# First layer's gate: the last 22 blocks' products made in row tiles of 64 and of 32 rows

## The chip, the cores and the metric

The kernel runs on one core of a Trainium2 chip. A core has TensorE (matrix products, PE in the profile; its weight loads are listed apart as PEld), VectorE (DVE), ScalarE (ACT), GpSimd (POOL) and SyncE (SP), which work through queues of their own, and 16 DMA engines that move data between the memory of the chip and the on-chip buffer. TensorE writes its results to PSUM, which this kernel uses as eight banks of 128 partitions by 512 float32 numbers. The metric is the time of one execution in microseconds (us).

## The reference, cut to what matters

The program is a two-layer transformer-like model on 256 tokens and 256 context tokens of width 2048. The first layer is a Fourier mixer with a gate:

```
def _fourier_branch(h, w_in, w_mix):
    u, z = jnp.split(h @ w_in, 2, axis=-1)          # each [512 tokens, 4096] with the context
    ...                                             # f: FFT over tokens and groups of u, then a mix
    return f * jax.nn.silu(z)

h = _rmsnorm(x, norm_g[i]) * (1 + scale) + shift
y = _fourier_branch(h, fnet_w_in[j], fnet_w_mix[j])
x = x + gate * (y @ w_out[i])
```

The change touches how `z = h @ w_in[:, 4096:]` is computed for 22 of its 32 blocks of 128 columns. Each block is a product of a 2048 x 128 piece of the weight, transposed, with h transposed (2048 x 512, both token sets side by side). The sum over the 2048 rows is made as 16 steps (k) of 128 rows. Everything is float32 in the reference. The second layer is an attention with a gate, and then a last norm.

## The kernel before, in words

All products of the gate are made in TensorE's fp32r format. To keep the precision, each operand is split in a high part (the value cast to fp32r) and a low part (what the cast left), and a product is three matmuls: high by high, high by low, low by high. The helper `mm3` (lines 78 to 81) issues these three, and so nearly all of TensorE's work stands on lines 79, 80 and 81 in the profile. The helper `half_split` (from line 67) makes the split of 128x1024 weights: the cast on ScalarE (L69, tile `wh`) and the subtraction on VectorE (L70, tile `wl`). The split halves live in the pool `ws`, six buffers, so three halves (high and low each). The raw weights come through the pool `raw`, three buffers of 128x2048.

The gate has 32 blocks, numbered b. Six are made early in the kernel and stored (`zd`), four beside each other in the stage ahead of the change, and the last 22 (b = 10 to 31) in a loop of their own. That loop is what changes. Per block it

- loads one raw weight tile of 128x2048 (SP queue) and splits it in two halves (`ws_split`);
- loads the Fourier part `ys[b]` from DRAM, after the weight's DMA;
- takes one PSUM bank and runs 16 steps of `mm3` into it, 48 matmuls of 128 rows (K), 128 columns of weights and 512 moving columns. The operand h is kept as 16 pairs `hs[k]` of a high and a low 128x512 tile, some in the pool `hx`, the others in `act`, so the profile calls the tiles `hx` or `act`;
- calls `z_out(b, o)`: a Silu on ScalarE from PSUM into a tile `z` (L703), the product `y = y * z` on VectorE (L704), and one or two pieces of another job, `next(ada)`.

The job `ada` (L666) is the conditioning product for later stages. It is made on VectorE with fused multiply-and-sum instructions on 128x1024 pieces of weights, which come through the same three `raw` buffers. It fills VectorE's time beside the gate and goes on in the stage behind it, the first layer's output projection. That stage starts with eight PSUM banks.

The order of the instructions on each engine is made by a planner, which goes by the program's order and by simulated times; `tc.issue_after` ties some instructions behind others. In each engine's queue the order is then fixed.

Three other places are named in the prediction. Line 320 and line 1220 use TensorE in tiles smaller than the array. Line 1220 (`stage_o`, in the second layer) is the value product of the attention:

```
for b in range(16):
    for hh in range(2):
        for g in range(4):
            q = slice(g * 32, g * 32 + 32)
            PE.matmul(oo[g][hh * 64 : hh * 64 + 64, 0:N], vrep[0][q, b, :], pall[q, hh, b].rearrange(...), start=b == 0, stop=b == 15)
```

There each matmul has 32 rows (partitions q) and 64 columns of weights, with four positions of rows (g) and two of columns (hh), in plain float32, for which the trace has two records a matmul (128 matmuls a stage, eight stages, 2048 records). Line 1015 is a 128x128 transpose in float32, also with two records each.

Of the kernel before, what the change touches and what calls it, by code (L numbers as in the profile page):

```python
# [10 lines left out]
F32 = mybir.dt.float32  # L11
F32R = mybir.dt.float32r
AF = mybir.ActivationFunctionType
ALU = mybir.AluOpType
AX = mybir.AxisListType

P = 128
D = 2048
KT = D // P
# [10 lines left out]
def tile_dit(ctx: ExitStack, tc: tile.TileContext, a: dict, out: bass.AP):  # L30
    nc = tc.nc
    V, S, PE, GP = nc.vector, nc.scalar, nc.tensor, nc.gpsimd
# [8 lines left out]
    def psum():  # L41
        return pp.tile([P, 512], F32, tag="ps", name="ps")
# [35 lines left out]
    def mm3(o, wh, wl, xh, xl, start, stop):  # L78
        PE.matmul(o, wh, xh, start=start, stop=False)  # L79
        PE.matmul(o, wh, xl, start=False, stop=False)  # L80
        return PE.matmul(o, wl, xh, start=False, stop=stop).ins  # L81
# [98 lines left out]
    with tc.tile_pool(name="st", reuse_waits="tile", bufs=1, side="right") as st, ExitStack() as sts:  # L180
# [306 lines left out]
        for i in range(4):  # L487
            for j in range(4):
                k = 4 * i + j
# [38 lines left out]
    for i in range(2):  # L528
        t = act(F32R).rearrange("p (k c) -> p k c", c=64)
# [149 lines left out]
    with tc.tile_pool(name="yp", reuse_waits="tile", bufs=32) as ypool:  # L679
        ys = []  # L680
        for b in range(NB):
            y = ypool.tile([P, 512], F32, tag="y", name="y")
            ys.append(y)
        hs = []
        hs_end = [None] * 3

        def make_hs(k):
            xt = act()
            hs_end[2] = nc.gpsimd.dma_start(xt, a["xT"][:, k, :]).ins
            h, l = h_tile(k), h_tile(k)  # L690
            for s in range(2):
                q = slice(s * N, (s + 1) * N)
                t = xt[:, q]
                V.scalar_tensor_tensor(t, t, gs0[:, k, s : s + 1], r_bc[:, q], op0=ALU.mult, op1=ALU.mult)
                hs_end[1] = S.activation(h[:, q], t, AF.Identity, bias=sh0[:, k, s : s + 1]).ins
                hs_end[0] = V.scalar_tensor_tensor(l[:, q], t, sh0[:, k, s : s + 1], h[:, q].bitcast(F32), op0=ALU.add, op1=ALU.subtract).ins
            hs.append((h, l))

        with tc.tile_pool(name="zp", reuse_waits="tile", bufs=2) as zp:
            def z_out(b, o):  # L700
                y = ys[b]
                z = zp.tile([P, 512], F32, tag="z", name="z")
                S.activation(z, o, AF.Silu)  # L703
                V.tensor_tensor(y, y, z, op=ALU.mult)  # L704
                if b >= NE + 4:
                    with tc.issue_after(hs_end[0]) if b < NE + 8 else nullcontext():
                        for _ in range(2 if b % 4 == 2 else 1):
                            next(ada)

            o4 = [psum() for _ in range(4)]  # L710
            for kg in range(4):
                wr = rawp.tile([P, D], F32, tag="raw", name="raw")
                last_dma[0] = nc.sync.dma_start(wr.rearrange("p (b c) -> p b c", b=4), a["wz"][NE - 4 : NE, :, kg * 512 : (kg + 1) * 512].rearrange("b p c -> p b c")).ins
                w = []
                for i in range(2):
                    make_hs(kg * 4 + i * 2)
                    with tc.issue_after(hs_end[0]) if kg else nullcontext(), tc.issue_after(hs_end[1]) if kg else nullcontext():
                        w.append(half_split(wr, i))
                    make_hs(kg * 4 + i * 2 + 1)
                for j in range(4):  # L720
                    k = kg * 4 + j
                    for b in range(4):
                        wh, wl = w[b // 2]
                        q = slice((b % 2) * 512 + j * P, (b % 2) * 512 + (j + 1) * P)
                        mm3(o4[b], wh[:, q], wl[:, q], hs[k][0], hs[k][1], k == 0, k == KT - 1)
            for b in range(NE + 4):
                with tc.issue_after(last_dma[0]):
                    nc.sync.dma_start(ys[b], fd[b])
            for b in range(4):
                z_out(NE + b, o4[b])  # L730
            for b in range(NE):
                z = zp.tile([P, 512], F32, tag="z", name="z")
                with tc.issue_after(last_dma[0]):
                    nc.sync.dma_start(z, zd[b])
                V.tensor_tensor(ys[b], ys[b], z, op=ALU.mult)
            for b in range(NE + 4, NB):
                w = ws_split(raw(a["wz"][b - 4]))
                with tc.issue_after(last_dma[0]):
                    nc.sync.dma_start(ys[b], fd[b])
                o = psum()  # L740
                for k in range(KT):
                    wh, wl = w[k // 8]
                    q = slice((k % 8) * P, (k % 8 + 1) * P)
                    mm3(o, wh[:, q], wl[:, q], hs[k][0], hs[k][1], k == 0, k == KT - 1)
                z_out(b, o)


        x1, sqs = [], []
        yy = {}

        def y_split0(i):
            for j in range(2):
                h, l = hxt(F32R), hxt(F32R)
                split(h, l, ys[i % 16 * 2 + j])
                yy[i, j] = (h, l)

        def evac0(k, o):
            t = xin.pop(0)
            for s in range(2):
                q = slice(s * N, (s + 1) * N)  # L760
                e = V.scalar_tensor_tensor(t[:, q], o[:, q], gt0[:, k, s : s + 1], t[:, q], op0=ALU.mult, op1=ALU.add).ins
            x1.append(t)
            t2 = hxt()
            with tc.issue_after(kv_w[0]) if k == 8 else nullcontext():
                sq_end[0] = S.activation(t2, t, AF.Square).ins
            if k in (13, 14):
                late.append(t2)
            elif 0 < k < 15:
                V.tensor_tensor(sqs[0], sqs[0], t2, op=ALU.add)
            else:  # L770
                sqs.append(t2)
            if k == 15:
                with tc.issue_after(e):
                    for t2 in late:
                        add_end[0] = V.tensor_tensor(sqs[0], sqs[0], t2, op=ALU.add).ins

        late, sq_end, add_end, kv_w = [], [None], [None], []
        xin = []
        ada_rate = {2: 2, 5: 2, 8: 2, 11: 2, 15: 0, 16: 0, 19: 2, 22: 2, 25: 2, 28: 2, 30: 0, 31: 0}
        y_split0(0)  # L780
        for i in range(32):
            sw, kg = i // 16, i % 16
            if kg == 0:
                o = [psum() for _ in range(8)]
            w = ws_split(raw(a["wo0"][sw, kg]))
            if i < 31:
                y_split0(i + 1)
            if kg >= 12:
                for k in range(sw * 8 + (kg - 12) * 2, sw * 8 + (kg - 12) * 2 + 2):
                    t = act()  # L790
                    nc.gpsimd.dma_start(t, a["xT"][:, k, :])
                    xin.append(t)
            for _ in range(ada_rate.get(i, 1)):
                next(ada)
            if i == 31:
                kv_raw = raw(a["wkv"][0])
                kv_h = wsp.tile([P, 1024], F32R, tag="ws", name="wh")
                kv_l = wsp.tile([P, 1024], F32R, tag="ws", name="wl")
                kv_w.append(S.copy(kv_h, kv_raw[:, 0:1024]).ins)
            if i == 24:  # L800
                S.activation(junk[:, 0:1], epsd, AF.Sqrt)
            edge = kg in (0, 15)
            for j, b in [(j, b) for b in range(8) for j in range(2)] if edge else [(j, b) for j in range(2) for b in range(8)]:
                q = slice(b * P, (b + 1) * P)
                mm3(o[b], w[j][0][:, q], w[j][1][:, q], *yy[i, j], kg + j == 0, kg * 2 + j == NB - 1)
                if kg == 15 and j == 1:
                    evac0(sw * 8 + b, o[b])
# [18 lines left out]
    o = psum()  # L826
# [12 lines left out]
    o = psum()  # L839
# [17 lines left out]
    for s in range(2):  # L857
        o = psum()[:, 0:N]
# [28 lines left out]
    with tc.tile_pool(name="h1", reuse_waits="tile", bufs=16) as h1p:  # L887
        hx1 = []
        kT = []
        with tc.tile_pool(name="kvp", reuse_waits="tile", bufs=2) as kvp:  # L890
            hc1 = []
            for k in range(KT):
                hx = h1p.tile([P, 512], F32R, tag="h1", name="h1")
                hc = kvp.tile([P, 512], F32R, tag="h1c", name="h1c", bufs=16)
                t = kvp.tile([P, 512], F32, tag="ht", name="ht")
                for s, h in ((0, hx), (1, hc)):
                    q = slice(s * N, (s + 1) * N)
# [10 lines left out]
            o = [[psum() for _ in range(2)] for _ in range(4)]  # L908
            for kg in range(8):
                w = [(kv_h, kv_l)] if kg == 0 else ws_split(raw(a["wkv"][kg]))  # L910
                for j in range(2):
                    k = kg * 2 + j
# [3 lines left out]
                    wh, wl = w[j]  # L916
                    for tb in range(4):
                        h = (hx1, hc1)[tb // 2][k]
                        c = (tb % 2) * P
                        for kv in range(2):  # L920
                            q = slice(kv * 512, (kv + 1) * 512)
                            mm3(o[tb][kv], h[:, c : c + P], h[:, N + c : N + c + P], wh[:, q], wl[:, q], k == 0, k == KT - 1)
            kr = []
            for tb in range(4):
                t = kvp.tile([P, 512], F32, tag="v", name="v", bufs=4)
# [3 lines left out]
                t = kvp.tile([P, 512], F32, tag="kr", name="kr", bufs=4)  # L929
# [5 lines left out]
            for hp in range(4):  # L935
                o = psum()
                for tb in range(4):
                    PE.transpose(o[:, tb * P : (tb + 1) * P], kr[tb][:, hp * P : (hp + 1) * P], ident)
                t = act()
# [7 lines left out]
        with tc.tile_pool(name="ye", reuse_waits="tile", bufs=6) as yep, ExitStack() as ats:  # L947
# [344 lines left out]
            with tc.tile_pool(name="fin", reuse_waits="tile", bufs=1) as fp:  # L1292
# [41 lines left out]
                o = [[psum() for _ in range(2)] for _ in range(2)]  # L1334
# [171 lines left out]
```

## Time and profile before

| | us |
|---|---|
| median of 3 runs | 1796.85 |
| lowest, highest | 1794.87, 1797.44 |
| the profiled execution's time | 1795.95 |
| its span, first to last instruction | 1794.2 |
| stage of blocks 10 to 20, from 423.0 | 122.4 |
| stage of blocks 21 to 31, from 545.4 | 122.9 |
| PE, DVE, ACT busy, share of the span | 99%, 77%, 49% |

Times in the trace are counted from the span's start. A row of the groups reads: line, engine, operation, tile written <- tiles read, shape, count | busy us, mean ns of one | idle time of the engine just ahead of them and what ended it. A "form" row gives the shortest, the median and the longest duration in ns. Durations of matmuls and weight loads are latencies and overlap; how often one starts tells the pace. The chain of work that ended last lists what the end of the kernel hung on, in order of time.

### The profile page before, as it was taken

To read this page: it belongs to the slowest core of one execution; us is meant where nothing else is said; L and a number is where in the kernel's file an instruction comes from. 1 tells how busy PE (TensorE), PEld (TensorE's weight loads), DVE (VectorE), ACT (ScalarE), POOL (GpSimd) and SP (SyncE) were. 2 spreads that over 40 slices of the span, in tenths; PEclk is the share of its full clock that TensorE was granted. 3 is DMA by queue.
4 is the path that set the end of the run, shared out by engine and by line. 5 is a ranking of instruction groups with operands and counts; after the bars stand their busy time and mean duration, and the time that the engine had idled before them with its cause. 6 is when DMAs were issued, how large, how long until landed. Compare 5 with 4: busy or idle time off the path is not lost.

```text
span 1794.2 us, 28006 instructions
## 1 busy us (share of the span) xinstructions
PE 1769.7 (99%) x10941; PEld 1486.6 (83%) x10941; DVE 1377.9 (77%) x2314; ACT 880.4 (49%) x1530; POOL 184.2 (10%) x224
## 2 busy tenths in 40 slices
PE   8999999999999999999999999999999999999997
PEld 6669999987888888888888888888888888887886
DVE  5769999978897887696976473788888878877454
ACT  6546444543322232323332353677778767866343
POOL 0001000020000010000000001033213312301010
PEclk9999999999999999999999999999999999999999
DMA  9985555476766676654576233544344343346543
GB/s 387 420 367 176 210 200 193 165 281 233 294 254 237 252 273 254 255 211 164 190 263 224 91 141 113 187 158 151 133 153 151 144 146 138 142 165 239 195 168 137
DMA packets 69028, 370.20 MB, mean 206 GB/s; under 512 B 8736, under 2 KB 10928, under 8 KB 35360
## 3 DMA queue, kind: packets, MB, share of 16 engines
q1 hardware_dynamic: 55344, 328.51, 48.9%
q0 software_dynamic: 9520, 32.96, 5.3%
q10 hardware_dynamic: 4032, 6.95, 1.1%
q8 instruction: 86, 1.41, 0.3%
q14 instruction: 46, 0.38, 0.1%
HBM read 353.16 MB, written 15.21 MB: 205 GB/s over the span
## 4 chain that ended last, share of the span: by engine, by line
PE 97%; ACT 1%; DMA 1%; DVE 0%; issue 0%; SPq 0%; DVEq 0%; ACTq 0%
PE ps L79 26%; PE ps L81 26%; PE ps L80 25%; PE ps L1142 7%; PE ps L1220 3%; PE ps L1144 3%; PE ps L320 2%; PE ps L1173 2%; PE ps L1174 2%; PE ps L1015 0%; DMA xn<-in_x 0%; DMA x1d<-act 0%; PE ps L629 0%; PE ps L600 0%; PE ps L336 0%
## 5 line engine op out<-in xcount | busy, mean ns | idle before, releaser
L69 ACT CAST wh<-raw 128x1024 fp32r<-128x1024 f32 x178 | 186.7, 1052 | 410.3 <-PE ps L80 377.6
L70 DVE TENSOR_TENSOR wl<-raw,wh 128x1024 fp32r<-128x1024 f32 x178 | 220.1, 1238 | 146.3 <-ACT wh L69 145.8
L79 PE MATMUL ps<-hx,wh 128*128 128x512 f32 x700 | 274.5, 394 | 0.0
L81 PE MATMUL ps<-hx,wl 128*128 128x512 f32 x700 | 273.1, 393 | 0.0
L80 PE MATMUL ps<-hx,wh 128*128 128x512 f32 x700 | 273.0, 390 | 0.0
L1092 DVE TENSOR_TENSOR wl<-raw,wh 128x1024 fp32r<-128x1024 f32 x142 | 190.6, 1348 | 39.2 <-ACT wh L1086 37.6
L1142 PE MATMUL ps<-h,wh 128*128 128x512 f32 x512 | 184.0, 399 | 0.0
L666 DVE CUSTOM_DVE_ANT_0 raw<-raw,cb 128x1024 f32<-128x1024 f32 x128 | 154.8, 1219 | 30.9 <-DMA raw<-in_adw 30.2
L1086 ACT CAST wh<-raw 128x1024 fp32r<-128x1024 f32 x142 | 148.8, 1049 | 59.0 <-PE ps L80 34.2
L81 PEld LDWEIGHTS ps<-hx,wl 128*128 128x128 f32 x700 | 131.4, 188 | 31.0
L80 PEld LDWEIGHTS ps<-hx,wh 128*128 128x128 f32 x700 | 131.4, 188 | 29.6
L79 PEld LDWEIGHTS ps<-hx,wh 128*128 128x128 f32 x700 | 131.5, 188 | 27.8 <-ACT hx L405 0.8
L1144 PE MATMUL ps<-h,wl 128*128 128x256 f32 x512 | 138.6, 281 | 0.0
L666 DVE CUSTOM_DVE_ANT_0 junk<-raw,cb 128x1024 f32<-128x1024 f32 x96 | 117.1, 1220 | 22.4 <-DMA raw<-in_adw 12.5
L80 PE MATMUL ps<-wl,h 128*128 128x512 f32 x320 | 125.2, 391 | 0.0
L81 PE MATMUL ps<-wh,h 128*128 128x512 f32 x320 | 124.9, 392 | 0.0
L79 PE MATMUL ps<-wh,h 128*128 128x512 f32 x320 | 124.5, 396 | 0.2 <-ACT h L899 0.2
L1191 ACT ACTIVATE p<-ps,mx 128x512 f32<-128x512 f32 x128 | 86.8, 683 | 75.0 <-DVE mx L1182 74.4
L1142 PEld LDWEIGHTS ps<-h,wh 128*128 128x128 f32 x512 | 96.1, 188 | 21.4
L1144 PEld LDWEIGHTS ps<-h,wl 128*128 128x128 f32 x512 | 96.6, 189 | 3.0
L81 PE MATMUL ps<-act,wl 128*128 128x512 f32 x234 | 91.0, 394 | 0.7 <-DVE wl L70 0.7
L1182 DVE CUSTOM_DVE_ANT_0 ps<-ps,mask,nsink 128x512 f32<-128x512 f32 x128 | 91.1, 752 | 0.5
(366 smaller groups left out, 4014.2 us busy)
## 6 DMA issues: line engine op xcount, KB each, us to landing
raw<-in_adw SPq DMA_DIRECT2D x64, 1024.0 KB, 4.9
raw<-in_wz SPq DMA_DIRECT2D x58, 1024.0 KB, 4.8
raw<-in_awp SPq DMA_DIRECT2D x32, 1024.0 KB, 12.4
raw<-in_wo SPq DMA_DIRECT2D x32, 1024.0 KB, 4.8
raw<-in_wq SPq DMA_DIRECT2D x32, 1024.0 KB, 4.8
raw<-in_wu SPq DMA_DIRECT2D x25, 1016.0 KB, 4.9
raw<-in_wo1b SPq DMA_DIRECT2D x16, 1024.0 KB, 4.8
act<-in_xT POOLq DMA_DIRECT2D x32, 256.0 KB, 5.1
```

The costliest lines, as they stand in the source:

```text
L69: cast[0] = S.copy(h, t[:, i * 1024 : (i + 1) * 1024]).ins
L70: V.tensor_tensor(l, t[:, i * 1024 : (i + 1) * 1024], h.bitcast(F32), op=ALU.subtract)
L79: PE.matmul(o, wh, xh, start=start, stop=False)
L80: PE.matmul(o, wh, xl, start=False, stop=False)
L81: return PE.matmul(o, wl, xh, start=False, stop=stop).ins
L666: V.tensor_tensor_reduce(junk if s == 0 and i < 3 else wf, wf, cb[:, s], 1.0, 0.0, ALU.mult, ALU.add, acc[:, i, kh, fg * 2 + f, s : s + 1])
L1086: cast[0] = S.copy(h, t[:, i * 1024 : (i + 1) * 1024]).ins
L1092: V.tensor_tensor(ready[n][1], ready[n][2], ready[n][0].bitcast(F32), op=ALU.subtract)
L1142: PE.matmul(o[0], wh[:, q], hx1[k], start=k == 0, stop=k == KT - 1)
L1144: PE.matmul(o[0][:, 0:N], wl[:, q], hx1[k][:, 0:N], start=False, stop=False)
L1182: V.tensor_tensor_reduce(so[tb], so[tb], mask[:, tb, :], -0.125, nsink[:, i : i + 1], ALU.add, ALU.min, mx[:, tb : tb + 1])
L1191: S.activation(pt[:, tb, :], so[tb], AF.Exp, bias=mx[:, tb : tb + 1], scale=-1.0, accum_out=sm[:, tb : tb + 1])
```

## The change

In the loop over the last 22 blocks, the 128 rows of each step k are cut in pieces of n rows: two of 64 rows for b = 10 to 20, four of 32 rows for b = 21 to 31. Each piece has a PSUM bank of its own and sums its own rows over all 16 steps. For each of the three products of a step, the pieces follow one another, so that neighbouring matmuls use different rows of the array. The three products and their order stay the same. At the end of a block ScalarE copies the first bank to a new tile `zt` in the on-chip buffer (one buffer), VectorE adds the others to it one by one, and `z_out` works on `zt` instead of PSUM.

```diff
                 with tc.issue_after(last_dma[0]):
                     nc.sync.dma_start(ys[b], fd[b])
-                o = psum()
+                n = 64 if b < 21 else 32
+                o = [psum() for _ in range(P // n)]
                 for k in range(KT):
                     wh, wl = w[k // 8]
                     q = slice((k % 8) * P, (k % 8 + 1) * P)
-                    mm3(o, wh[:, q], wl[:, q], hs[k][0], hs[k][1], k == 0, k == KT - 1)
-                z_out(b, o)
+                    for j, (wx, hx_) in enumerate(((wh, hs[k][0]), (wh, hs[k][1]), (wl, hs[k][0]))):
+                        for i, oi in enumerate(o):
+                            rows_ = slice(i * n, (i + 1) * n)
+                            PE.matmul(oi, wx[rows_, q], hx_[rows_], start=k == 0 and j == 0, stop=k == KT - 1 and j == 2)
+                t = zp.tile([P, 512], F32, tag="zt", name="zt", bufs=1)
+                S.copy(t, o[0])
+                for oi in o[1:]:
+                    V.tensor_tensor(t, oi, t, op=ALU.add)
+                z_out(b, t)
```

Per block this is 96 matmuls of 64 rows, or 192 of 32 rows, in place of 48 of 128 rows, each with 128 columns of weights and 512 moving columns, two or four PSUM banks in place of one, one more ScalarE instruction, and one or three more on VectorE. Loads from DRAM are unchanged.

## The prediction

> **What bounds the kernel now.** I read the page first: the busy shares, the granted clock and the chain of work that ended last.
>
> ```profile
> span 1794.2 us, 28006 instructions
> PE 1769.7 (99%) x10941; PEld 1486.6 (83%) x10941; DVE 1377.9 (77%) x2314; ACT 880.4 (49%) x1530; POOL 184.2 (10%) x224
> PEclk9999999999999999999999999999999999999999
> PE 97%; ACT 1%; DMA 1%; DVE 0%; issue 0%; SPq 0%; DVEq 0%; ACTq 0%
> ```
>
> 97% of the chain is TensorE at a full clock, so a nanosecond added to each product of a stage is a nanosecond of the kernel, and the other engines matter only where they make TensorE wait. Next, the windows of the two stages that change (columns: length, busy us and instruction count of PE, weight loads, DVE, ACT, POOL; clock, DMA share, GB/s), the first the 64-row blocks, the second the 32-row blocks:
>
> ```profile
> 423.00:545.40 122.40, 121.71 (x525) 98.30 (x524) 105.22 (x157) 33.53 (x39) 0.54 (x1) 1.00 0.71 268
> 545.40:668.30 122.90, 122.90 (x531) 99.54 (x530) 101.47 (x152) 35.35 (x42) 7.17 (x14) 1.00 0.67 254
> ```
>
> Eleven blocks of 48 matmuls are 528, and 122.90/531 gives 231.5 ns from one to the next: 11.1 us a block. VectorE is busy for 101 of 123 us here, so it is the engine to watch.
>
> **Are row tiles worked on side by side?** The 22 blocks keep their 1056 products but issue each as two (528 x 2 = 1056) or four (528 x 4 = 2112) matmuls of as many columns. If the pieces ran one after the other they would cost a full pass each. The kernel already has one place with row tiles: line 1220, 32 rows by 64 columns, four row tiles times two column tiles. Its rows in the chain, and those of full-array float32 transposes (L1015) and of full-array products beside it:
>
> ```profile
> 1143.99 0.87 PE ps L1015 x8
> ...
> 1200.37 0.23 PE ps L79
> ...
> 1203.77 0.23 PE ps L1173
> ...
> 1204.68 7.72 PE ps L1220 x256
> 1212.40 0.43 PE ps L79
> ```
>
> A float32 record on the full array takes 0.87/8 = 109 ns for 128 moving columns, so 218 ns for the 256 of line 1220. 256 of them in turn would be 55.8 us; they took 7.72, 7.2 at a time. Two column tiles alone give two at a time and four row tiles alone four, so both work together here. That is the row nearest to the change, and by it I take two 64-row pieces, and four 32-row pieces, for the price of one full product.
>
> **Are their weight loads hidden too?** A load comes with every matmul, so the change doubles or quadruples the loads, each still of 128 columns. The forms (min/median/max ns):
>
> ```profile
> L1220 PEld LDWEIGHTS ps<-pall,vr x2048: 127/132/132, 1204.6 to 1642.4; 32*64 32x64 f32 x187
> L1220 PE MATMUL ps<-pall,vr x2048: 371/374/425, 1204.6 to 1642.6; 32*64 32x256 f32 x187
> L81 PEld LDWEIGHTS ps<-act,wl x234: 186/188/188, 379.9 to 667.4; 128*128 128x128 f32 x117
> L81 PE MATMUL ps<-act,wl x234: 387/393/497, 380.1 to 667.7; 128*128 128x512 f32 x117
> ```
>
> These are latencies that overlap, so only their pace says what a load occupies. Line 1220 did 256 loads of 64 columns in 7.72 us: 30.2 ns each, or 60.3 ns for 128 columns, even if one loader served all tiles. Four such loads are 241 ns against 231.5: nearly hidden if they were strictly serial, wholly if row tiles load side by side. The other end comes from the widest pace of a 128-column load for these fp32r products, beside matmuls of 256 columns:
>
> ```profile
> 142.99 0.28 PE L81 MATMUL ps<-hx,wml 128*127 128x256 f32 x1
> ...
> 143.94 0.28 PE L80 MATMUL ps<-act,wmh 128*127 128x256 f32 x1
> ```
>
> Nine starts, eight steps in 0.95 us: 119 ns, so a load occupies at most that. Two in turn are 238 ns (6 ns too many), four 475 ns (244 too many). Ends: 0 and 528 x 6 + 528 x 244 = 3 + 129 = +132 us. I take 0, because line 1220 has the same 32-row tiles and already moves 512 weight columns in 241 ns.
>
> The Trainium skill, "TensorE: Matmul & The Clock Gate", section "The mechanism" of Part 3, speaks against the change: a weight load overlaps a running matmul only when the row group differs. By that each tile would pay a load and then a stream, 60 + 231.5 ns at the least, some +64 us over 1056 products. The trace disagrees: line 1220's eight tiles each had 256/8 = 32 records in 7.72 us, 241 ns a record, where the stream alone is 218 and a serial load at the bound would bring it to 278.
>
> **Mode changes.** The first product after line 1220 stands at 0.43 us in the chain, the others at 0.23: 0.20 us for one change of tile shape. There are three (128 to 64 rows, 64 to 32, back to 128): **+0.6 us**. Ends 0 and 3 x 0.43 = 1.3.
>
> **What the sum of the pieces adds.** Each block gains one ScalarE copy of 128x512 out of PSUM and one (64-row) or three (32-row) VectorE adds from PSUM, and the Silu then reads SBUF instead of PSUM. Nearest rows, and the present work of the 32-row stage:
>
> ```profile
> L822 ACT COPY act<-ps 128x512 f32<-128x512 f32 x8 | 4.4, 583 | 2.1 <-DMA x1d<-act 2.0
> L1307 DVE TENSOR_TENSOR act<-ps,gbc 128x512 f32<-128x512 f32 x7 | 4.5, 682 | 8.0 <-PE ps L81 8.0
> L703 ACT ACTIVATE z<-ps 128x512 f32<-128x512 f32 x11 | 6.6, 596 | 30.0 <-PE ps L81 30.0
> L666 DVE CUSTOM_DVE_ANT_0 junk<-raw,cb 128x1024 f32<-128x1024 f32 x28 | 34.2, 1220 | 4.5 <-DMA raw<-in_adw 2.6 <-ACT cb L659 1.9
> L666 DVE CUSTOM_DVE_ANT_0 raw<-raw,cb 128x1024 f32<-128x1024 f32 x27 | 32.9, 1219 | 0.3
> L70 DVE TENSOR_TENSOR wl<-raw,wh 128x1024 fp32r<-128x1024 f32 x22 | 26.9, 1222 | 14.8 <-ACT wh L69 14.8
> L704 DVE TENSOR_TENSOR y<-y,z 128x512 f32<-128x512 f32 x11 | 7.6, 687 | 3.8 <-ACT z L703 3.8
> ```
>
> ScalarE: 11 x 0.58 = 6.4 us a stage on an engine busy for 35 of 123 us; nothing. VectorE, 64-row stage: 11 x 0.68 = 7.5 us into 122.4 - 105.2 = 17.2 us of free time. 32-row stage: 33 x 0.68 = 22.5 us into idle time of 4.5 + 0.3 + 14.8 + 3.8 = 23.4 us. That nearly fills VectorE. Most of that idle time is spare, for it waits on ScalarE's cast, which waits on TensorE. Behind the adds in VectorE's queue stand the low halves of the weights (L70), which TensorE needs, and behind the Silu in ScalarE's queue the next cast (L69). Their lead:
>
> ```profile
> 489.72 1.05 ACT L69 CAST wh<-raw 128x1024 fp32r<-128x1024 f32 x1 [4.51 <-PE ps L80]
> ...
> 495.30 1.05 ACT L69 CAST wh<-raw 128x1024 fp32r<-128x1024 f32 x1 [2.23 <-PE ps L80]
> ```
>
> Casts come 5.6 us apart, each released by TensorE's last read of a half. The six weight buffers hold three halves (high and low), so a half is wanted two halves later: 11.1 us, less 1.05 for the cast and 1.22 for L70, leaves 8.8 us. The new chain at a block's end (copy 0.58, three adds 2.05, Silu 0.60) delays a cast by at most 3.2 us and leaves 5.6 for VectorE to lag. I take **+2 us** of TensorE waiting; ends 0 (the lead holds) and 22.5 + 7.5 = 30 (none of the idle time usable). The first blocks have less lead. There TensorE already waited for L70 once:
>
> ```profile
> 428.90 0.50 PE L81 MATMUL ps<-act,wl 128*128 128x512 f32 x1 [0.69 <-DVE wl L70]
> ```
>
> That is in block 10, before its add, so it stays. PSUM: four banks a block in eight banks give each block 11.1 us to be copied and added (2.6 us), and the output projection behind starts on the four banks of block 30 (4 x 6 x 0.23 = 5.5 us of cover).
>
> **Sum.** The profiled execution took 1795.95 us (span 1794.2, 1.75 around it). 1795.95 + 0.6 + 2 = 1798.6; the median shown, 1796.85, is 0.9 above that execution, so 1799.4, say **1799 us**.
>
> **The rivals.**
>
> *One loader for all tiles.* The loads of row tiles take turns, at a price between the two paces, 60 and 119 ns. For: no row shows 128-column fp32r loads in row tiles. Against: line 1220's pace. It decides above 231.5/4 = 58 ns in the 32-row blocks, above 116 in the 64-row ones. Midway, at 90 ns, four are 360: 528 x 128 = 68 us, 1867 us; the end is 1799 + 132 = 1931.
>
> The Trainium skill, "TensorE: Matmul & The Clock Gate", "Measured speedup vs the span model", gives four row tiles of 32 rows and 512 columns a speedup of 3.07, not 4: an estimate of 1.30 products a set, 528 x 70 ns = +37 us, 1836. No run here shows that shape; 1.30 sets is a load of 75 ns in this rival.
>
> *The tiles take turns.* Row tiles of full 128-column width, fp32r, don't overlap: (1 + 3) x 528 x 231.5 ns = +489 us, 2288 us. For it only that line 1220 differs in type and width.
>
> *Faster: the gap between products goes.* From 256 columns in 119 ns and 512 in 226.7 (fifteen products from 1200.37 to 1203.77) a column costs 0.42 ns, so 512 stream in 215 and 16.5 of the 231.5 are gap. If tiles fill one another's gaps, 1056 x 16.5 = 17.4 us come back: 1782. For: line 1220's 7.2 at a time out of 8 includes its two ends, so it loses little in between. Against: a tile's own next product still has its own gap. From 6 ns of gap won, the kernel is faster beyond the noise.
>
> *VectorE becomes the bound.* The waits in its queue stay where they are and half of the 30 us is exposed: 1812 us. For: 22.5 into 23.4. Against: the lead of 5.6 us a half.
>
> *Instructions come late.*
>
> ```profile
> PE ps L1220 <- issue: 3.8, 3, 1.6
> q8 instruction: 86, 1.41, 0.3%
> ```
>
> The 2 x 10941 TensorE records over 86 packets are 254 each. At line 1220 a packet lasted 3.8 us and TensorE stood still three times in eight such stages, 1.6 us at the longest. The 32-row blocks issue 384 instructions in 11.1 us, a packet in 7.4: twice the time. If each of their 17 packets stalled 1.6 us: +27, 1826 us.
>
> **How the numbers follow.** Side by side, as summed: 0.50, its own range 1794 to 1806. One loader 0.20. Turns 0.12. Faster 0.10. VectorE 0.05, instructions 0.03. A measurement of this kernel tells about 0.2% (3.6 us) from no change. Faster by more: 0.09 of the gap rival, 0.02 of the forecast: 0.11. Within: 0.30 of the forecast, 0.01: 0.31. Slower: 0.18 of the forecast and all of the other four (0.40): 0.58. The range leaves out the turns (0.12) and the full gain of the gap (0.05) and goes from 1788 to 1926.
>
> **What will show it.** Both windows at 122 to 125 us with 1056 and 2112 matmuls of 64 and 32 rows: the step on tiles holds. The first unchanged and the second long, with evenly spaced matmuls: the loader. Twice and four times as long: turns. Shorter windows: the gap. TensorE waiting on L70 or on the new adds: VectorE. My weakest step is the load: fp32r loads in row tiles appear nowhere in this trace.

## The result and the profile after

The changed kernel took **1960.33 us** (median of 3 runs, 1959.86 to 1960.48) against 1796.85: 1.0912 times as long, 95% interval 1.0887 to 1.0937. That is 161 us above the forecast of 1799 and outside its range. The profile of the changed kernel, first the page's lines for the span, the busy time, the granted clock in 40 slices and the chain that ended last:

```profile
span 1958.5 us, 32285 instructions
PE 1820.0 (93%) x13053; PEld 1518.6 (78%) x13053; DVE 1410.9 (72%) x2358; ACT 887.8 (45%) x1552; POOL 184.6 (9%) x224
PEclk9999999998888878889999999999999999999999
PE 56%; issue 7%; DVE 6%; DMA 4%; ACT 1%; DVEq 0%; ACTq 0%; POOLq 0%
```

The clock is no longer full in slices 10 to 18 (441 to 881 us), which is where the change lies, and the chain that was 97% TensorE is now broken by VectorE and DMAs. The same window view as before, for the 64-row stage, the 32-row stage, and the start of the output projection behind them:

```profile
417.00:608.00 191.00, 147.46 (x1083) 114.82 (x1082) 117.21 (x176) 36.25 (x47) 0.80 (x2) 0.87 0.49 176
608.00:814.30 206.30, 150.32 (x2116) 119.57 (x2112) 120.52 (x177) 34.98 (x45) 7.48 (x14) 0.85 0.45 156
814.30:844.00 29.70, 11.31 (x33) 7.42 (x33) 20.11 (x33) 6.63 (x11) 0.54 (x1) 0.69 0.47 161
```

**Where the 164.3 us lie** (span 1794.2 to 1958.5). The two stages took 245.3 us before, from 423.0 on. They take 397.3 now, from 417.0 on, since the first products of block 10 are mixed with those of the block ahead: 152.0 - 6.0 us. The projection then stands still for 29.7 - 11.3 = 18.4 us. Together 164.4. Within the 397.3 us TensorE is idle for 43.5 + 56.0 = 99.5. At full pace the work in them is 245.3 + 6.0 = 251.3; the other 46.5 us are products at less than full pace.

**The row tiles themselves keep the pace forecast.** TensorE's timeline, one stretch in each stage (columns: start, duration, then the instruction; x4 are four neighbours drawn together):

```profile
602.60 0.63 PE L748 MATMUL ps<-act,wh 64*128 64x512 f32 x4
603.06 0.40 PE L748 MATMUL ps<-act,wl 64*128 64x512 f32 x2
603.29 0.63 PE L748 MATMUL ps<-hx,wh 64*128 64x512 f32 x4
...
612.22 0.64 PE L748 MATMUL ps<-hx,wh 32*128 32x512 f32 x8
612.69 0.40 PE L748 MATMUL ps<-hx,wl 32*128 32x512 f32 x4
612.92 0.63 PE L748 MATMUL ps<-act,wh 32*128 32x512 f32 x8
```

A step k, three products, goes from 602.60 to 603.29 and from 612.22 to 612.92: 0.69 and 0.70 us, 0.23 a product, whether it comes in two pieces or in four. Before it was 231.5 ns. From the starts of all sets in the trace, the median is 233 ns for pairs and for sets of four, those just behind a wait included; in the run with the order held (below) it is 232 for both, as in the kernel before, read in the same way.

**What TensorE waits for.** The waits between 415 and 860 us (us in all, times, longest), some rows of the list:

```profile
ACT z L703 <- DVE zt L752: 302.1, 21, 23.0
DVE junk L666 <- DMA raw<-in_adw: 128.2, 27, 7.1
PE ps L748 <- DVE wl L70: 44.9, 14, 10.6
PE ps L748 <- DVE zt L752: 43.8, 19, 11.8
PE ps L79 <- DVE zt L752: 13.6, 1, 13.6
PEld ps L748 <- issue: 1.4, 4, 0.4
```

TensorE waits for VectorE: for the low halves of weights (L70) and for the adds (L752) that free its PSUM banks. VectorE has work for only 117 and 121 us of these long stages; it waits itself, 128 us in all, at a conditioning piece (L666) for weights. (One `next(ada)` loads one tile of weights and works it off in four instructions on L666; "piece" below is one of these four.) VectorE's timeline in the middle of the two stages shows the order in which this happens:

```profile
594.54 1.22 DVE L70 TENSOR_TENSOR wl<-raw,wh 128x1024 fp32r<-128x1024 f32 x1
595.68 0.68 DVE L752 TENSOR_TENSOR zt<-ps,zt 128x512 f32<-128x512 f32 x1
597.06 0.69 DVE L704 TENSOR_TENSOR y<-y,z 128x512 f32<-128x512 f32 x1 [0.70 <-ACT z L703]
598.00 1.23 DVE L70 TENSOR_TENSOR wl<-raw,wh 128x1024 fp32r<-128x1024 f32 x1 [0.24 <-ACT wh L69]
604.16 1.23 DVE L666 CUSTOM_DVE_ANT_0 junk<-raw,cb 128x1024 f32<-128x1024 f32 x1 [4.94 <-DMA raw<-in_adw]
...
607.84 1.22 DVE L666 CUSTOM_DVE_ANT_0 raw<-raw,cb 128x1024 f32<-128x1024 f32 x1
609.22 1.22 DVE L70 TENSOR_TENSOR wl<-raw,wh 128x1024 fp32r<-128x1024 f32 x1
610.46 0.68 DVE L752 TENSOR_TENSOR zt<-ps,zt 128x512 f32<-128x512 f32 x1
```

and SyncE's queue (two issues of loads drawn as one row), the total of what its loads waited for on L70 from 415 to 860 us, and TensorE:

```profile
599.25 10.18 SPq L47 DMA_DIRECT2D raw<-in_adw  x2
```

```profile
SPq L47 <- DVE wl L70: 100.8, 24, 14.9
```

```profile
595.82 0.50 PE L748 MATMUL ps<-hx,wl 64*128 64x512 f32 x2 [3.23 <-DVE wl L70]
...
610.49 0.51 PE L748 MATMUL ps<-hx,wl 32*128 32x512 f32 x4 [1.50 <-DVE wl L70]
```

Read it as a ring. The low half at 598.00 ends at 599.23 and is the last reader of its `raw` buffer. At 599.25 SyncE issues the load of conditioning weights into a `raw` buffer. VectorE has that load's piece next in its queue and stands still until 604.16. It works off four pieces (4.9 us) and only then makes the low half at 609.22, for which TensorE has been waiting, and the add at 610.46, for which the Silu has been waiting on ScalarE and, behind the Silu, the next cast. Then the ring starts anew. A turn is 609.22 - 594.54 = 14.7 us, where a block of products is 11.1.

Not every turn is like this one. In some VectorE stands before two such loads, one behind the other:

```profile
679.07 1.23 DVE L666 CUSTOM_DVE_ANT_0 junk<-raw,cb 128x1024 f32<-128x1024 f32 x1 [5.05 <-DMA raw<-in_adw]
...
688.87 1.23 DVE L666 CUSTOM_DVE_ANT_0 junk<-raw,cb 128x1024 f32<-128x1024 f32 x1 [4.89 <-DMA raw<-in_adw]
```

Between the Silu at 452.07 and the last at 845.83 lie 21 turns. Twelve with one load take 14.4 to 16.0 us, 50 us more in all than twelve blocks at 11.1; seven with two loads take 18.1 to 28.4, 94 us more; two with a wait for `cb`, the vector that the pieces are multiplied with, 17 more. So over half of the loss is in the seven turns with two loads.

### The profile page after: what moved, and what is told of

The parts are those of the page before. It is cut to its first block, busy times and chain, and to the rows that moved or that the text cites. A ratio compares the mean times of both kernels' runs of the same rounds, so it can differ in the third digit from the quotient of the medians.

```text
span 1958.5 us, 32285 instructions
## 1 busy us (share of the span) xinstructions
PE 1820.0 (93%) x13053; PEld 1518.6 (78%) x13053; DVE 1410.9 (72%) x2358; ACT 887.8 (45%) x1552; POOL 184.6 (9%) x224
## 4 chain that ended last, share of the span: by engine, by line
PE 56%; issue 7%; DVE 6%; DMA 4%; ACT 1%; DVEq 0%; ACTq 0%; POOLq 0%
PE ps L79 13%; PE ps L81 13%; PE ps L80 13%; PE ps L1150 6%; DMA raw<-in_adw 4%; PE ps L1228 3%; PE ps L1152 3%; DVE junk L666 2%; PE ps L1181 1%; PE ps L1182 1%; DVE wl L70 1%; DVE raw L666 1%; DVE zt L752 1%; PE ps L748 1%; DMA cb<-in_crow 0%
## 5 line engine op out<-in xcount | busy, mean ns | idle before, releaser
L70 DVE TENSOR_TENSOR wl<-raw,wh 128x1024 fp32r<-128x1024 f32 x178 | 220.9, 1242 | 120.8 <-ACT wh L69 120.8
L666 DVE CUSTOM_DVE_ANT_0 junk<-raw,cb 128x1024 f32<-128x1024 f32 x96 | 117.3, 1222 | 164.6 <-DMA raw<-in_adw 138.1
L79 PE MATMUL ps<-hx,wh 128*128 128x512 f32 x546 | 216.2, 399 | 18.3 <-DVE zt L752 13.6
L81 PE MATMUL ps<-hx,wl 128*128 128x512 f32 x546 | 214.6, 395 | 0.0
L80 PE MATMUL ps<-hx,wh 128*128 128x512 f32 x546 | 214.2, 392 | 0.0
L666 DVE CUSTOM_DVE_ANT_0 raw<-raw,cb 128x1024 f32<-128x1024 f32 x128 | 155.3, 1222 | 48.0 <-DMA raw<-in_adw 46.0
L748 PE MATMUL ps<-hx,wh 32*128 32x512 f32 (+1 forms) x924 | 139.8, 443 | 48.4 <-DVE zt L752 43.8
L748 PE MATMUL ps<-act,wh 32*128 32x512 f32 (+1 forms) x1188 | 152.2, 413 | 6.2 <-ACT wh L69 6.2
L703 ACT ACTIVATE z<-zt 128x512 f32<-128x512 f32 x22 | 13.9, 631 | 312.3 <-DVE zt L752 302.1
L748 PEld LDWEIGHTS ps<-hx,wh 32*128 32x128 f32 (+1 forms) x924 | 86.7, 211 | 71.8 <-DVE zt L752 53.7
L79 PEld LDWEIGHTS ps<-hx,wh 128*128 128x128 f32 x546 | 103.9, 190 | 41.4 <-DVE zt L752 14.0
L81 PEld LDWEIGHTS ps<-hx,wl 128*128 128x128 f32 x546 | 103.7, 190 | 25.0 <-DVE wl L70 0.8
L80 PEld LDWEIGHTS ps<-hx,wh 128*128 128x128 f32 x546 | 103.7, 190 | 23.5 <-DVE hx L62 0.5
L748 PEld LDWEIGHTS ps<-act,wh 32*128 32x128 f32 (+1 forms) x1188 | 103.1, 199 | 23.8 <-ACT wh L69 7.0
```

The source lines that it names most:

```text
L70: V.tensor_tensor(l, t[:, i * 1024 : (i + 1) * 1024], h.bitcast(F32), op=ALU.subtract)
L666: V.tensor_tensor_reduce(junk if s == 0 and i < 3 else wf, wf, cb[:, s], 1.0, 0.0, ALU.mult, ALU.add, acc[:, i, kh, fg * 2 + f, s : s + 1])
L748: PE.matmul(oi, wx[rows_, q], hx_[rows_], start=k == 0 and j == 0, stop=k == KT - 1 and j == 2)
```

## The experiments

Where no interval is given, a time is that of one run; twelve runs of the kernel before lay between 1793.73 and 1797.06 us. Each row of order strings below lists one engine's queue over three or four of the 32-row blocks. VectorE: `w` a low half (L70), `a` a conditioning piece (L666), `+` an add, `y` the product behind the Silu (L704). ScalarE: `C` a cast, `K` the copy out of PSUM, `Z` the Silu.

Two theories stand at the head. A: the Silu, which used to wait for TensorE only, now waits in ScalarE's queue for VectorE's adds, and holds up the casts behind it. B: the queues are in another order than before, in which the low halves and adds stand behind conditioning pieces that wait for loads. A third, plainer one is that the sum's own work is too much for VectorE. In all experiments line numbers below the edit shift by a few.

### The sum left out

```diff
-                t = zp.tile([P, 512], F32, tag="zt", name="zt", bufs=1)
-                S.copy(t, o[0])
-                for oi in o[1:]:
-                    V.tensor_tensor(t, oi, t, op=ALU.add)
-                z_out(b, t)
+                z_out(b, o[0])
```

> The row tiles stay, two of 64 and four of 32 rows, but the copy to zt and the adds are left out: the Silu reads the first bank alone, so the gate holds only the first piece's rows (the sum over the other pieces is what this kernel leaves out). Theory A, the new wait: ScalarE's Silu now waits for VectorE's adds, and the casts that feed TensorE stand behind it in ScalarE's queue. Without the sum that wait is gone: 1796 to 1806 us. Theory B, the order: the planner, which the trace shows to have packed the conditioning job ahead of a block's second low half, made an order that fits a slower TensorE, and it is this order that starves TensorE. The order here is nearly that of the changed kernel, with the adds left out, so most of the loss stays: 1880 to 1960 us. Theory C, VectorE has too much work: 30 us of adds are gone, so near 1800.

1925.72 us, against 1794.57 for the kernel before beside it. With no copy, no add and no wait of the Silu for an add, 131 of the 165 us are still lost. Its waits from 415 to 850 us:

```profile
DVE junk L666 <- DMA raw<-in_adw: 138.0, 27, 7.2
PE ps L748 <- DVE wl L70: 79.2, 21, 11.5
```

So neither the sum nor its wait is the main cause.

### The sum made, but not read

```diff
                 for oi in o[1:]:
                     V.tensor_tensor(t, oi, t, op=ALU.add)
-                z_out(b, t)
+                z_out(b, o[0])
```

> As the changed kernel with its copy and adds, but the Silu reads the first bank in PSUM and nobody reads zt (the gate leaves the other pieces out). VectorE has all of its new work, ScalarE's Silu no longer waits for it. Theory A: the loss goes, 1797 to 1815 us. Theory B: most of it stays, 1880 to 1960. Theory C (VectorE's work): it stays as it was, 1940 to 1965.

1945.27 us. The copies and adds bring 20 us over the kernel without them, the Silu's wait for them another 15; VectorE stands still for conditioning loads as long as before (132.2 us in 27 waits).

### The whole array, with the same sum behind it

```diff
-                z_out(b, o)
+                t = zp.tile([P, 512], F32, tag="zt", name="zt", bufs=1)
+                S.copy(t, o)
+                for _ in range(1 if b < 21 else 3):
+                    V.tensor_tensor(t, o, t, op=ALU.add)
+                z_out(b, t)
```

This edit is made to the kernel before.

> The products as before on the full array in one bank, but with the copy to zt, one add (blocks 10 to 20) or three adds (21 to 31) of that same bank to zt, and the Silu reading zt: the new chain and the new VectorE work without row tiles (the gate is computed from a multiple of z, which leaves its value wrong). Theory A: the wait of the Silu on VectorE is there, so most of the loss is: 1880 to 1960 us. Theory B: the order is made for a TensorE that takes 11.1 us a block, as it does: 1797 to 1815. Theory C: 1940 to 1965.

1793.68 us against 1794.57. The stages of this kernel:

```profile
423.00:545.40 122.40, 121.71 (x526) 98.26 (x525) 109.07 (x164) 39.68 (x48) 0.54 (x1) 1.00 0.69 260
545.40:668.30 122.90, 122.90 (x531) 99.51 (x530) 113.77 (x175) 40.88 (x51) 7.25 (x14) 1.00 0.68 254
```

Every copy, every add and the Silu's wait for the adds are there, VectorE works 113.8 of 122.9 us, and TensorE has no idle time at all in the second stage. Both A and the plain theory fall. What differs from the changed kernel is the products, and the order of the queues. VectorE and ScalarE, this kernel and then the changed one:

```
full array + sum  +aa+waaw+aay+aa+waaw+aay+aa+wwa+ay    KCCZKCCZKCCZ
row tiles         w++ywaaaa+w++ywaaaa+w++ywaaaaaaaa+    CCKZCCKZCCKZ
```

In the first row pieces come one or two at a time between low halves and adds. In the changed kernel four or eight come in one run, ahead of the block's first add.

### The Silu issued behind the next block's casts

```diff
+                if held_z:
+                    with tc.issue_after(cast[0]):
+                        z_out(*held_z.pop())
...
-                z_out(b, t)
+                held_z.append((b, t))
```

The sum gets three buffers with it, in the pool of `z`, and the Silu works in place there.

> The changed kernel with its whole sum, but the Silu, the product with y and the conditioning pieces of block b are issued behind the casts of block b+1, in a tile of their own (three buffers, Silu in place). Theory A: the casts no longer stand behind a Silu that waits for VectorE, so most of the loss goes: 1800 to 1850 us. Theory B: the order on VectorE is still made for a slow TensorE (four conditioning pieces ahead of the second low half): 1880 to 1960.

1950.86 us: 9 of 164 us come back. That the Silu stands ahead of casts is a small part. The waits for conditioning loads remain:

```profile
DVE junk L666 <- DMA raw<-in_adw: 118.0, 25, 8.2
PE ps L752 <- DVE z L756: 56.5, 20, 20.2
```

### Row tiles in one stage alone

```diff
-                n = 64 if b < 21 else 32
+                n = 64 if b < 21 else 128
```

> Row tiles with their copy and add in blocks 10 to 20 alone, two of 64 rows; blocks 21 to 31 as before the change. Theory B: this part carries what the first stage lost in the changed kernel, about 60 to 80 us: 1855 to 1880.

```diff
-                n = 64 if b < 21 else 32
+                n = 128 if b < 21 else 32
```

> Row tiles with their copy and adds in blocks 21 to 31 alone, four of 32 rows; blocks 10 to 20 as before the change. Theory B: about 80 to 100 us: 1875 to 1900.

In both, a block of n = 128 takes the one bank to `z_out` without a sum. 1869.87 us for the 64-row stage alone (+75), 1905.15 for the 32-row stage alone (+110, 5 us above the expectation). Pieces of 64 rows, with one add a block, cost two thirds of what pieces of 32 rows do with three: the price doesn't follow the number of adds. The two sum to 185, 20 more than both together, so the parts are not independent; the second also has the projection's wait of 13.4 us, which the first hasn't.

### The order exchanged

For these, each recorded instruction of the two engines is tied to the one that stood ahead of it in another kernel's queue, which adds no wait between engines:

```diff
+    for start, seq in ORDERS:                  # one string for ScalarE, one for VectorE
+        at_, prev = dict(start), None
+        for c in seq:
+            ins = REC[c][at_[c]]
+            at_[c] += 1
+            if prev is not None:
+                tc.add_manual_dep(ins, prev.name, NoSync, reason="order")
+            prev = ins
```

Row tiles in the order of the full-array kernel with the sum, for blocks 10 to 28:

> The changed kernel with all of its products, copies and adds, but ScalarE's and VectorE's instructions of blocks 10 to 28 (casts, copies, Silus; low halves, adds, conditioning pieces, products with y) are held in the order that the planner had given to the same instructions beside products on the full array (the run with the sum and full-array products, 1793.7 us). Blocks 29 to 31 stay in the changed kernel's order. Theory B, the order is the cause: 1795 to 1815 us, and TensorE's pace in both stages is that of before. Rival D, it takes both, the pieces and the sum (the full-array run was fast because it has no pieces): over 1850 us.

1832.2 us (1829.94 to 1837.47), 1.0204 times before (1.0187 to 1.0221), above the 1815 expected. Blocks 10 to 28 now run at the pace of before; the first wait of TensorE beyond 10 us begins at 660.9. What is left stands in the last three blocks and the projection's start, whose order was left as it was:

```profile
PE ps L81 <- DVE zt L754: 13.7, 1, 13.7
PE ps L750 <- DVE zt L754: 12.9, 4, 10.3
```

The reverse, full-array products with the same sum, in the changed kernel's order for blocks 10 to 28:

> The opposite exchange: products on the full array with the copy and the adds of one bank (the gate is computed from a multiple of z, which leaves its value wrong), ScalarE and VectorE of blocks 10 to 28 held in the changed kernel's order. No row tile is left. Theory B: 1900 to 1965 us. Rival D: 1795 to 1830.

1930.37 us: +135 without one row tile in these blocks. Its windows over the stretches used for the changed kernel, and its waits:

```profile
417.00:608.00 191.00, 148.20 (x557) 113.30 (x556) 118.81 (x178) 36.25 (x47) 0.81 (x3) 0.87 0.47 176
608.00:814.00 206.00, 147.24 (x574) 114.89 (x575) 130.66 (x194) 43.42 (x57) 7.99 (x15) 0.87 0.47 171
```

```profile
DVE junk L668 <- DMA raw<-in_adw: 111.3, 25, 7.3
PE ps L83 <- DVE wl L71: 90.2, 24, 15.2
```

In the first window this kernel gets through 557 products, the changed one through 554.5 (26 of the block ahead and 1057 halves), and the clock and, to 2%, the busy time of every engine agree. One bank a block in place of four moves the waits from the adds to the low halves, but the loss stays.

Then the good order to the end of the gate and through the first steps of the projection, with the three adds of blocks 29 to 31 kept together:

> As the run with the changed kernel's work in the full-array order, but held in that order to the end: blocks 29 to 31 and the first steps of the output projection too (the three adds of each of blocks 29 to 31 are drawn together, since a bank they free is needed earlier than with one bank a block). Theory B: the 36 us that the first such run still lost came after 660 us, in the blocks left in the changed kernel's order, so they go: 1795 to 1803 us, the time of before within about 0.4%. Rival D, the pieces and their sum cost something of their own beside the order: over 1810 us.

**1799.58 us** (median of 9 runs, 1797.82 to 1806.33), 1.0030 times before (1.0019 to 1.0041). This is the whole change, all row tiles and sums, and it takes about what the prediction's sum gives. Its stages, and its longest waits of TensorE:

```profile
423.00:545.40 122.40, 122.40 (x1045) 104.65 (x1045) 108.56 (x162) 39.66 (x48) 0.53 (x1) 1.00 0.71 258
545.40:668.30 122.90, 120.67 (x2060) 103.93 (x2061) 110.73 (x172) 38.14 (x47) 4.64 (x9) 1.00 0.67 245
```

```profile
PE ps L81 <- ACT zt L752: 3.0, 1, 3.0
PE ps L750 <- DVE zt L754: 2.2, 2, 1.2
PE ps L83 <- DVE wl L71: 1.7, 1, 1.7
```

### No conditioning pieces in the gate

The changed kernel in the planner's own order, with the 28 conditioning tiles of the gate's loop left out, their loads and four pieces each (the first 28 are skipped where the job makes them, and their sums set to zero, which the lines below leave out):

```diff
-                if b >= NE + 4:
-                    with tc.issue_after(hs_end[0]) if b < NE + 8 else nullcontext():
-                        for _ in range(2 if b % 4 == 2 else 1):
-                            next(ada)
```

> The changed kernel without the 28 conditioning pieces (L666, with their weights' loads) that stood beside blocks 10 to 31 (the conditioning product lacks them, so what is computed later is wrong); the planner is free. Theory B1, what hurts in the order is that VectorE's queue waits for a conditioning piece's load, whose buffer the low halves ahead of it in the same queue set free: without the pieces nothing waits for such a load, 1790 to 1810 us. Theory B2, the order hurts without them as well, since the low halves stand behind adds and Silus that come late: over 1840 us.

1816.16 us, 6 above the expectation, but 144 of the 165 us are gone. From 461.7 to 550.8 and from 563.9 to 641.8 the Silus come 11.13 us apart, eight and seven blocks on end. The longest wait that remains is the one at the projection's start, where block 31's adds stand behind eight conditioning pieces that were not left out:

```profile
PE ps L79 <- DVE zt L755: 12.9, 1, 12.9
```

### What makes the order

Full-array products issued two or four times over, with the sum:

```diff
-                    mm3(o, wh[:, q], wl[:, q], hs[k][0], hs[k][1], k == 0, k == KT - 1)
+                    n = 2 if b < 21 else 4
+                    for r_ in range(n):
+                        mm3(o, ..., k == 0 and r_ == 0, k == KT - 1 and r_ == n - 1)
```

> Products on the full array, each issued two times (blocks 10 to 20) or four times (21 to 31) into one bank, with the copy and the adds (so the gate is computed from a multiple of z and its value is wrong). The order that the planner gives this kernel's ScalarE and VectorE is nearly that of the changed kernel. If that order was made for pieces that take turns, it fits a TensorE that is really that slow: TensorE waits little and the time is 1796 + 489 = 2285, 2275 to 2300 us. If the order is bad in itself, the same waits as in the changed kernel come on top or in part: over 2320.

2273.45 us, 478.6 more than before for 2112 added products, just under the range expected: 227 ns each, so nothing beside the products costs anything. The queue it gets is nearly the changed kernel's:

```
full array, issued 4x  w+++ywaaaaw+++ywaaaaw+++y
row tiles              w++ywaaaa+w++ywaaaa+w++y
```

Here the waits run the other way, ScalarE for TensorE:

```profile
ACT wh L69 <- PE ps L80: 318.4, 30, 21.0
```

and TensorE has no gap above 0.5 us in the stage. So that order fits a TensorE that needs two or four passes a block. That the planner reckons row tiles as passes in turn is inferred from the likeness of the two orders and not shown: its own simulated times for them are not on record.

## Why the prediction was wrong

- **Row tiles side by side, +0: right.** 232 ns a set with the order held, for pairs and for fours, against 231.5 (forecast's first step), and the rival of tiles in turn is out. The Trainium skill, "TensorE: Matmul & The Clock Gate", "Measured speedup vs the span model", has 3.07 for four row tiles of 512 columns; here four tiles go in the 232 ns of one full product, 4.0 over a long run of sets, so by this trace the +37 us estimated from it don't exist.
- **Weight loads hidden, 0 of an end of +132: right.** Four loads of 128 columns come with each 232 ns, and the spacing doesn't grow from two to four. One loader at 60 to 119 ns a load is out, and its 1867 us as well; whether the four run side by side or in turn at 58 ns or less, no run tells. The comparison at line 1220 (278 against 241 ns) decided less than the prediction says: 60 ns is the bound for 128 columns, and for the 64 of that line it is 30, which makes 248.
- **Mode changes, +0.6: small, not separately measured.** One step from 128 to 64 rows stands 0.32 us behind the last where 0.23 is usual: 0.1 us. There are more than three, because block 10 starts between products of the block ahead.
- **Faster by the gap: out**, no gain where 6 ns were needed. **Instructions late: out**, 1.4 us in four waits.
- **The step that failed is the sum's: "delays a cast by at most 3.2 us and leaves 5.6 for VectorE to lag. I take +2 us".** The size was wrong by 160 us, and so was the thing that was sized. I counted VectorE's added work against its idle time, and took the order of its queue and the lead of 8.8 us from the trace of before. The added work was indeed free: the full-array kernel with the sum is at 1793.68. But the queue was ordered anew, and the lead is a property of the order. With a run of four pieces and their load ahead of a low half, that half comes 5 + 4.9 us later, and 8.8 is gone. The row of L666 that I quoted, with 4.5 us of idle time, 2.6 of them ended by the load of `raw`, held the warning: a piece of conditioning waits for a load into one of three shared buffers, and whatever stands behind it in the queue waits too. I counted these 4.5 us as idle time to be filled. With two loads and eight pieces ahead of it, as in the seven long turns, the half comes about twice as late.
- **PSUM, put at nothing: failed with the order.** The prediction gave each block 11.1 us for its copy and adds and the projection 5.5 us of cover. TensorE waited 43.8 us for adds that free banks in the stages, and 13.6 us at the projection's start for those of block 31, which stand behind eight pieces and their loads.
- **The rival "VectorE becomes the bound", 1812 us,** named the right engine and waits (L70 and the adds, as "What will show it" said), but not the mechanism: VectorE is at 117 of 191 us, not full, and its bound of 30 us was made from busy time alone. 0.05 was too little for a change that multiplies the instructions from which a planner derives every queue.
- **With the order held, the sum comes out nearly**: 1.0030 (1.0019 to 1.0041) against its 1.0014 (2.6 us of 1796), so a few us more than it had; TensorE's waits in that run are 6.9 us from 415 to 860, where the sum put 2. That 1799.58 meets 1799 so closely is luck in part, for the kernel before took 1796.85 when the forecast was made and 1794.81 beside this run. Order alone costs 135 us (full array, changed order), and removing it gives back 160.8 of 165.5.
- **Open:** how the 46.5 us of products below full pace divide. 122 steps of 380 to 500 ns are 24 of them, at 0.19 us over; the rest was not split. Nor was one engine's order exchanged without the other's: that the late Silu gives back 9 us, and that TensorE waits for L70 and L752, speak for VectorE's queue. The run without conditioning tiles takes away their loads and their work together, so it doesn't say what each is worth.

## What to carry to other kernels

Where a planner orders the queues, a change of TensorE's instructions is also a change of every other engine's order: look for what could come to stand ahead of the work TensorE waits for, and price the longest wait of that (here a load of 5 us and 4.9 us of work, in some blocks twice) against the lead, not busy time against idle time. To tell a slow operation from a bad order, pin the old order onto the new operations and the new order onto the old ones. Row tiles of full width gain nothing for products that already fill 128 rows: they cost nothing on TensorE either, but bring copies, adds and PSUM banks.

## What the runs showed of the hardware

- Weight loads of 128 columns for four row tiles, with a 512-column product each, go at 232 ns a set. The prediction held the load for its weakest step.
- After longer waits the products themselves are slower for a while. Behind the wait of 3.23 us, in the changed kernel, the products and their window, in which the granted clock (third from the end) is 0.50:

```profile
597.01 1.06 PE L748 MATMUL ps<-act,wh 64*128 64x512 f32 x4
597.86 0.63 PE L748 MATMUL ps<-act,wl 64*128 64x512 f32 x2
598.29 1.06 PE L748 MATMUL ps<-hx,wh 64*128 64x512 f32 x4
```

```profile
596.67:600.08 3.41, 3.41 (x20) 2.67 (x18) 1.92 (x2) 2.72 (x4) 0.00 (x0) 0.50 0.79 327
```

Three products take 598.29 - 597.01 = 1.28 us here, 427 ns each, and 0.69 from 602.60 on. Behind the wait of 1.50 us at 610.49 the products keep 0.23, and so they do behind one of 3.02 us that ended at 543.80, while behind one of 3.05 us that ended at 464.38 they take 427 ns: the length alone doesn't decide it. So waiting is paid twice: 99.5 us of idle time in the stages came with 46.5 us of slower work, and the granted clock of 0.87 and 0.85 is a consequence of the waits and not a cause: with the order held it is 1.00 with the same row tiles. The Trainium skill, "TensorE: Matmul & The Clock Gate", "What's actually happening", says that the clock goes to half after an idle window of some 3.4 us and comes back after a busy one; the 427 against 232 ns agree with it, apart from the length, for a wait of 3.23 us was enough here.
